# Row sums with 128 columns of ones, a two-row product ahead of GpSimd's solve, and two 64-row halves that take turns

## The chip, the cores and the metric

The kernel runs on one core of a Trainium2 chip (trn2). The metric is the device time of one execution in microseconds (us); smaller is better. The engines are named as the profile names them: PE (TensorE matmul), PEld (its weight loads), DVE (VectorE), ACT (ScalarE), POOL (GpSimd), SP (SyncE, which issues most DMAs).

## What is computed

A decoder trunk of two layers for 256 tokens of width 1024, in float32. The reference, cut to what matters here:

```python
for l in range(DEPTH):                                   # DEPTH = 2
    h = h + 0.5 * swiglu_ffn(rms_norm(h, g[l, 0]), w_in[l, 0], w_out[l, 0])   # width 2816
    u = rms_norm(h, g[l, 1]); z = u @ mix_w_in[l]
    y_a = rwkv7_time_mix(z[..., :1792], ...)             # 8 heads of 64, a recurrence over tokens
    y_b = retention_mix(z[..., 1792:4864], ...)          # 8 heads, chunks of 128 tokens
    h = h + (gate_a * (y_a @ w_branch_a[l]) + gate_b * (y_b @ w_branch_b[l])) @ mix_w_out[l]
    h = h + memory_cross_attn(rms_norm(h, g[l, 2]), mem, ...)
    h = h + 0.5 * swiglu_ffn(rms_norm(h, g[l, 3]), w_in[l, 1], w_out[l, 1])
return rms_norm(h, final_norm)
```

The recurrence of `rwkv7_time_mix` is done in two chunks of 128 tokens. Within a chunk it needs products of keys with queries (scores, masked to the causal half), and the inverse of a unit triangular matrix for each head.

## The kernel before, in words

**Dense products.** Each weight block is fetched by an SP DMA (`raw`), cut by ACT into a rounded part `wh` and by DVE into the rest `wl` (lines 245 and 246), and PE then makes three products of hi and lo parts, a triple (`mm3`): hi by hi, hi by lo, lo by hi. Most are 128 x 128 weights against 256 columns (`unit_k`, `acc_t`; tiles g, u, acc, z, xq), some against 512 columns (`unit`; z). Some 90% of PE's instructions are such triples, one behind the other.

**The order.** PE's order is the one in which the program emits it. `Em` keeps a clock of its own, `em.now`, which each matmul advances by an assumed cost (`mm`), and small tasks cut into the dense stream when their times on that clock have come. So an assumed cost decides between which triples a small product stands. The other engines' orders come from a scheduler that starts from this program.

**Row sums.** `norm` runs ahead of each of the eight sublayers: two float32 matmuls of `ss` (squares, 128 x 128) by one column of `s.ones` add the squares of a token's row. The result `rb` goes through DVE, POOL (a power) and ACT, and comes back as a second pair of matmuls (`rb<-diagh`, `rb<-diagl`). `rw_low` has four such one-column products per layer (`dsc`). A float32 matmul is two instructions on PE.

**The solve.** `rw_chain` runs once per layer. PE makes scores `sc` of `be` and `al`, ACT copies them to `U`, SP DMAs carry them through DRAM (`ug`) into `us`, and POOL inverts 64 triangular blocks by 31 steps of a product and a sum (lines 1179 and 1180). Step k works on k // 2 + 1 rows of 31 - k elements, so from step 2 on it has two rows or more. `xs` starts as a constant (line 1171) that is loaded long before. The result goes through DRAM again (`xg`, `XB`), and PE needs `XB` for the first `SA` product, which stands in PE's queue behind a number of dense z products.

**The scores of keys.** `late(t)`, called for t = 0 ahead of that first `SA` and for t = 1 behind the first chunk, makes the products `sc<-mh,kh` and so on. Heads stand in pairs, one on partitions 0 to 63 and one on 64 to 127, so each product uses 64 rows of PE's array. The loop is over the half `o` outside, then over `i` and `pr`, with `mm3` inside: all 12 products of a half come together and the other half follows after some z products. DVE masks each bank into `S` (line 1143).

Of the kernel before, what the change touches and what calls it, by code (L numbers as in the profile page):

```python
# [13 lines left out]
AF = mybir.ActivationFunctionType  # L14
# [10 lines left out]
def make_consts():  # L25
    f = np.float32
    i = np.arange(P)
    c = {}
    c["ident"] = np.eye(P, dtype=f)
    # cum[s, t] = (s <= t) - (s <= 63): inclusive running sum centred on the middle of the chunk  # L30
    c["cum"] = (i[:, None] <= i[None, :]).astype(f) - (i[:, None] <= 63).astype(f)
    ms = np.zeros((P, 2, P), np.int32)
    ms[:, 0, :] = np.where(i[:, None] < i[None, :], -1, 0)
    ms[:, 1, :] = np.where(i[:, None] <= i[None, :], -1, 0)
    c["masks"] = ms
    half = CDEC * 0.5
    b = np.zeros((P, 8), np.float64)
    b[:, 0] = -half * (i - 63)
    b[:, 1] = half * (i - 63)
    b[:, 2] = -half * (i - 64)  # L40
    b[:, 3] = -CDEC * 64
    b[:, 4] = i >= 64
    b[:, 5] = i < 64
    b[:, 6] = -0.5
    c["cols"] = b.astype(f)
    lg = np.log1p(-np.exp2(-5.0 - np.arange(8, dtype=np.float64)))
    t = np.arange(256, dtype=np.float64)[:, None]
    gam = np.stack([np.exp(t * lg), 0.125 * np.exp(-t * lg)], 1)  # [256, 2, 8]
    c["gam"] = np.ascontiguousarray(gam.reshape(2, P, 2, 8).transpose(1, 0, 2, 3)).astype(f)
    # angles: inverse frequencies and 1/(2 pi) cut into four 12-bit pieces  # L50
    fr = (10000.0 ** (-np.arange(32) / 32)).astype(f)
    pieces = []
    from fractions import Fraction
    inv2pi = Fraction(15915494309189533576888376337251436203445964574046, 10 ** 50)
    r = inv2pi
    e = -3
    for _ in range(4):
        q = Fraction(int(r * Fraction(2) ** (11 - e)), 1) / Fraction(2) ** (11 - e)
        pieces.append(float(q))
        r -= q  # L60
        e -= 12
    c["freq"] = np.broadcast_to(np.concatenate([fr, fr]).astype(f), (P, 64)).copy()
    c["_pieces"] = pieces
    x0 = np.zeros((P, 16, 32), f)
    for p in range(P):
        for rr in range(16):
            x0[p, rr, 2 * rr + p // 64] = 1.0
    c["x0"] = x0
    return c
# [7 lines left out]
class Em:  # L77
    """Emits the program: the dense products are the main stream, the other tasks cut in when ready."""
# [83 lines left out]
class K:  # L162
# [63 lines left out]
    def hp(s, gen):  # L226
        """a task whose steps go before others on the other engines"""
        while True:
            with s.tc.high_priority():
                try:  # L230
                    y = next(gen)
                except StopIteration:
                    return
            yield y
# [57 lines left out]
    def unit(s, X, key, K, c, ps):  # L292
        """ps[t][128 tok, c] = x W for a block of columns of W, K row blocks."""
        k = 0
        while k < K:
            wh, wl = s.W.next(key)
            for j in range(wh.shape[1]):
                if X == s.Xu:
                    yield s.ev_u[k // 2]
                for t in range(2):  # L300
                    s.mm3(ps[t][:, :c], *X(t, k), wh[:, j, :], wl[:, j, :], k == 0, k == K - 1)
                yield 0
                k += 1
            s.W.done()

    def unit_k(s, X, key, K, nc_, ps):
        """ps[c // 2][:, c % 2] = (x W)^T for nc_ blocks of 128 columns: the weights stand, the tokens move.
        Two groups share a bank: its first product alone clears the bank."""
        k = 0
        while k < K:  # L310
            wh, wl = s.W.next(key)
            for j in range(wh.shape[1]):
                if X == s.Xt:
                    yield s.ev_u[k // 2]
                xh, xl = X(k)
                for c in range(nc_):
                    o = ps[c // 2][:, c % 2 * 256:c % 2 * 256 + 256]
                    cs = slice(c * P, (c + 1) * P)
                    s.mm3(o, wh[:, j, cs], wl[:, j, cs], xh, xl, k == 0 and c % 2 == 0, k == K - 1 and c % 2 == 1)
                    if c % 2:  # L320
                        yield 0
                k += 1
            s.W.done()

    def acc_t(s, X, key, k0, nk, acc, start):
        """acc[j][:, i] += (x[k0:k0+nk] W rows)^T for column blocks 2j + i, a chunk being one row block by 1024 columns."""
# [11 lines left out]
    def acc_t_last(s, parts, acc, done):  # L338
        """The last row blocks of an accumulation, bank by bank; done(j) follows each."""
# [14 lines left out]
    def acc_chunk(s, X, key, k0, nk, acc, start):  # L354
        """acc[t][n] += x[k0:k0+nk] W rows, by tokens"""
# [11 lines left out]
    def acc_last(s, parts, acc, scale):  # L367
        """the last row blocks, token tile by token tile, and the final norm"""
# [24 lines left out]
    def prep(s, j):  # L393
        """blocks 2j, 2j + 1 of h are final"""
# [29 lines left out]
    def norm(s, ss, ev, early, wait):  # L424
        """half of 1/rms, for the token of a partition and along the free axis of every partition"""
# [4 lines left out]
        for t in range(2):  # L430
            s.mm(b[:, t:t + 1], ss[:, 0, t * P:(t + 1) * P], s.ones[:, 0:1], True, True)
# [7 lines left out]
        with s.tc.high_priority():  # L439
            nc.vector.tensor_scalar(x, b[:, 0:2], 4.0 / D, 4e-6, ALU.mult, ALU.add)  # L440
# [35 lines left out]
    def start(s):  # L476
        """x transposed into the trunk, the first weights and the first u"""
# [36 lines left out]
    def hl(s, src, name):  # L514
        """[128, 512] -> hi and lo parts"""
# [11 lines left out]
    def transp(s, src, t, pr):  # L527
        """[128, 512] of tokens by columns -> the four transposed blocks in hi and lo parts (a PE step)"""
# [96 lines left out]
    def h_tok(s):  # L625
        """the trunk of the last sublayer, by tokens"""
# [53 lines left out]
    def fin(s, acc, scale):  # L680
        """done(j) for acc_t_last: blocks 2j, 2j + 1 of h get their sum"""
# [43 lines left out]
    def evac(s, ps, name, free=True):  # L725
        """z = u W with 1/rms applied, for both token tiles"""
# [138 lines left out]
    # RWKV-7: decay, gate and in-context rate from the low-rank columns  # L865
    def rw_low(s, l, ps):
# [85 lines left out]
        for b in range(4):  # L952
            s.mm(pd[:, b:b + 1], tm[:, b * P:(b + 1) * P], s.ones[:, 0:1], True, True)
        s.ar.free(tm)
        R["dsc"] = s.sm.tile([P, 4], F32, name="dsc", tag="dsce")
        act.activation(R["dsc"], pd[:, 0:4], AF.Exp, scale=-hc, bias=s.col(3))
# [17 lines left out]
    def shift(s, z):  # L974
        """the rows of the token before"""
# [10 lines left out]
    def shift_mix(s, z, zs, mu):  # L986
        """z + (z of the token before - z) mu, in place"""
# [143 lines left out]
    def scores(s, lT, rT):  # L1131
        """[s, t] products, the even heads in one bank and the odd heads in another"""
# [13 lines left out]
    def rw_chain(s, l):  # L1146
# [19 lines left out]
        # unit upper triangular 32 x 32 diagonal blocks inverted, one (token tile, head, block) and  # L1166
        # every other row to a partition
# [3 lines left out]
        nc.gpsimd.dma_start(xs, A["x0"])  # L1171
        for i in range(2):
# [18 lines left out]
        def late(t):  # L1191
# [18 lines left out]
            for o in range(2):  # L1210
# [3 lines left out]
                KQ[t][o] = []  # L1214
                p0, p1 = 64 * o, 64 * o + 64
                for i in range(2):
                    b = s.ps.alloc("sc")
                    for pr in range(2):
                        f = lambda x: x[p0:p1, pr].rearrange("p c t -> p (c t)")
                        s.mm3(b[:, pr * 256:pr * 256 + 256], kh[p0:p1, 2 * i + pr, :], kl[p0:p1, 2 * i + pr, :],  # L1220
                              f(mv[i][0]), f(mv[i][1]), True, True)
                    x = s.ar.alloc("S", F32, (P, 2, 2, P))
                    s.mask_evac(x, b, s.masks.unsqueeze(1).broadcast_to([P, 2, 2, P]))
# [89 lines left out]
    # retention  # L1313
# [121 lines left out]
    def mem_t(s):  # L1435
        """the memory times 1/rms of its rows, transposed, into DRAM"""
# [30 lines left out]
    def mem_prep(s, l):  # L1467
        """the normalised memory, transposed, in hi and lo parts: blocks of [128, 2, 256]"""
# [17 lines left out]
    def mem_v(s, n):  # L1486
        """half of the memory's values"""
# [47 lines left out]
    def x_scores(s, n, qT, kT, sc, pT, ev):  # L1535
        """softmax over the memory for heads 2n, 2n + 1, and its transpose"""
# [36 lines left out]
    def x_out(s, n, pT, vv, oT, evp, ev):  # L1573
        """the transposed output of heads 2n, 2n + 1 in hi and lo parts"""
# [98 lines left out]
```

## Time and profile before

| | |
|---|---|
| median of 3 runs | 1536.84 us (1536.01 to 1538.4) |
| profiled execution, first to last instruction (span) | 1535.5 us |
| PE busy | 98% of the span |
| DVE, ACT, POOL busy | 69%, 50%, 10% |
| granted TensorE clock, mean | 0.989 |

The profile shows one execution. Its own time beyond the span is not given; the runs that make the median were timed apart and lie 1.3 us above the span. A PE matmul row gives the start and a modelled duration that overlaps the next one; the pace of a stretch is read from the starts, or from the chain of waits, which gives the time of a stretch and the number of its matmuls.

### The profile page before, as it was taken

Reading aid. Unit: us, or ns where it says so; the run is one execution under the profiler, and the core shown is the slowest. Engines: PE = TensorE matmul, PEld = TensorE weight load, DVE = VectorE, ACT = ScalarE, POOL = GpSimd, SP = SyncE. Lnnn points to the kernel's source line nnn. Section 1 sums busy time; section 2 is a strip of 40 time slices with the busy share of each in tenths; the row PEclk is TensorE's granted clock in tenths of the full one; section 3 lists DMA queues with packets and bytes.
Section 4 is the critical chain, followed back from the end, with each engine's and each line's share of the span. In section 5 each row is a group of like instructions: output and inputs, shape, how many; then the busy total and the mean of one; then the engine's idle time right before and its main releaser. Section 6 shows DMA issues by size and latency. Waiting matters only on the chain.

```text
span 1535.5 us, 28618 instructions
## 1 busy us (share of the span) xinstructions
PE 1501.5 (98%) x11763; PEld 1427.0 (93%) x11763; DVE 1055.8 (69%) x1459; ACT 766.7 (50%) x1053; POOL 152.4 (10%) x229
## 2 busy tenths in 40 slices
PE   8999999989999999999999999999799999999998
PEld 8999988868999999999999999888699999999997
DVE  7966599947646767665685666899466477576664
ACT  6554465525434555444464444654354356464442
POOL 4010001370000000000001000205600000000000
PEclk9999999998999999999999999999899999999999
DMA  8677656525445545666567554564354454466661
GB/s 278 218 225 241 195 170 195 172 65 189 152 147 162 189 127 188 192 193 193 178 209 228 188 189 156 192 213 144 117 165 139 152 177 167 137 197 193 194 195 46
DMA packets 143066, 271.19 MB, mean 177 GB/s; under 512 B 22580, under 2 KB 35108, under 8 KB 142936
## 3 DMA queue, kind: packets, MB, share of 16 engines
q1 hardware_dynamic: 139560, 261.12, 52.9%
q0 software_dynamic: 2864, 7.63, 1.9%
q8 instruction: 92, 1.51, 0.4%
q10 hardware_dynamic: 512, 0.62, 0.1%
q14 instruction: 38, 0.31, 0.1%
HBM read 263.05 MB, written 3.15 MB: 173 GB/s over the span
## 4 chain that ended last, share of the span: by engine, by line
PE 89%; POOL 5%; DMA 2%; issue 1%; SPq 1%; DVE 1%; ACT 1%; POOLq 0%
PE z L211 25%; PE acc L211 21%; PE g L211 16%; PE u L211 16%; POOL tm L1179 3%; PE xq L211 3%; POOL xs L1180 2%; PE tp L223 1%; PE SA L211 1%; PE Y L211 1%; PE G L211 1%; PE xo L211 1%; PE xs L211 1%; SPq L1164 1%; PE sc L211 1%
## 5 line engine op out<-in xcount | busy, mean ns | idle before, releaser
L246 DVE TENSOR_TENSOR wl<-raw,wh 128x1024 fp32r<-128x1024 f32 x476 | 582.0, 1230 | 310.2 <-ACT wh L245 308.2
L245 ACT ACTIVATE wh<-raw 128x1024 fp32r<-128x1024 f32 x476 | 501.3, 1059 | 538.6 <-PE z L211 145.6
L211 PE MATMUL g<-uh,wh 128*128 128x256 f32 x704 | 196.8, 280 | 0.0
L211 PE MATMUL g<-uh,wl 128*128 128x256 f32 x704 | 196.5, 279 | 0.0
L211 PE MATMUL g<-ul,wh 128*128 128x256 f32 x704 | 196.5, 279 | 0.0
L211 PE MATMUL u<-uh,wh 128*128 128x256 f32 x704 | 196.3, 279 | 0.0
L211 PE MATMUL u<-uh,wl 128*128 128x256 f32 x704 | 195.8, 278 | 0.0
L211 PE MATMUL u<-ul,wh 128*128 128x256 f32 x704 | 195.7, 278 | 0.0
L211 PE MATMUL acc<-ah,wh 128*128 128x256 f32 x528 | 146.9, 278 | 0.0
L211 PE MATMUL acc<-ah,wl 128*128 128x256 f32 x528 | 146.8, 278 | 0.0
L211 PE MATMUL acc<-al,wh 128*128 128x256 f32 x528 | 146.8, 278 | 0.0
L211 PEld LDWEIGHTS g<-uh,wh 128*128 128x128 f32 x704 | 134.0, 190 | 0.2
L211 PEld LDWEIGHTS g<-uh,wl 128*128 128x128 f32 x704 | 133.1, 189 | 0.1
L211 PEld LDWEIGHTS g<-ul,wh 128*128 128x128 f32 x704 | 133.0, 189 | 0.2
L211 PEld LDWEIGHTS u<-uh,wh 128*128 128x128 f32 x704 | 132.9, 189 | 0.0
L211 PEld LDWEIGHTS u<-uh,wl 128*128 128x128 f32 x704 | 132.4, 188 | 0.0
L211 PEld LDWEIGHTS u<-ul,wh 128*128 128x128 f32 x704 | 132.3, 188 | 0.0
L211 PE MATMUL z<-wh,uh 128*128 128x512 f32 (+1 forms) x320 | 125.4, 392 | 0.0
L211 PE MATMUL z<-wh,ul 128*128 128x512 f32 (+1 forms) x320 | 122.4, 383 | 0.4 <-DVE ul L407 0.4
L211 PE MATMUL z<-wl,uh 128*128 128x512 f32 (+1 forms) x320 | 121.6, 380 | 0.0
L211 PEld LDWEIGHTS acc<-ah,wh 128*128 128x128 f32 x528 | 99.9, 189 | 0.0
L211 PEld LDWEIGHTS acc<-ah,wl 128*128 128x128 f32 x528 | 99.2, 188 | 0.0
(400 smaller groups left out, 3331.5 us busy)
## 6 DMA issues: line engine op xcount, KB each, us to landing
raw<-in_ffn_w_in SPq DMA_DIRECT2D x176, 512.0 KB, 4.4
raw<-in_mix_w_in SPq DMA_DIRECT2D x108, 512.0 KB, 4.4
raw<-in_ffn_w_out SPq DMA_DIRECT2D x88, 512.0 KB, 4.3
raw<-in_cross_w_kv SPq DMA_DIRECT2D x32, 512.0 KB, 3.6
raw<-in_w_branch_b SPq DMA_DIRECT2D x16, 512.0 KB, 3.6
raw<-in_mix_w_out SPq DMA_DIRECT2D x16, 512.0 KB, 3.6
raw<-in_cross_w_q SPq DMA_DIRECT2D x16, 512.0 KB, 3.9
raw<-in_cross_w_o SPq DMA_DIRECT2D x16, 512.0 KB, 4.2
```

The source lines that it names most:

```text
L211: s.nc.tensor.matmul(out, l, r, start=start, stop=stop)
L223: s.nc.tensor.transpose(out, src, s.ident)
L245: s.nc.scalar.activation(hi, src, AF.Copy)
L246: s.nc.vector.tensor_tensor(lo, src, hi.bitcast(F32), ALU.subtract)
L1164: nc.sync.dma_start(ugv[t, k][:, q], U[t][q][32 * k:32 * k + 32, :, 32 * k:32 * k + 32])
L1179: nc.gpsimd.tensor_tensor(tm[:, 0:nr, 0:w], xc, row, ALU.mult)
L1180: nc.gpsimd.tensor_tensor(xs[:, 0:nr, k + 1:32], xs[:, 0:nr, k + 1:32], tm[:, 0:nr, 0:w], ALU.add)
```

## The change

Three edits. In `norm` and `rw_low` the right operand `s.ones[:, 0:1]` becomes all 128 columns of `s.ones`, and the readers take every 128th column. Behind the load of `xs`, POOL runs one product of two rows by 29 elements on `xs`, written to `tm` where the solve overwrites it. In `late`, the loop over `i` is outside now and the loop over the half `o` innermost, so the products of the two halves alternate, in two banks; `em.now` is set back by 650 ns after each 12.

```diff
 in norm
-            s.mm(b[:, t:t + 1], ss[:, 0, t * P:(t + 1) * P], s.ones[:, 0:1], True, True)
+            s.mm(b[:, t * P:(t + 1) * P], ss[:, 0, t * P:(t + 1) * P], s.ones, True, True)
...
-            nc.vector.tensor_scalar(x, b[:, 0:2], 4.0 / D, 4e-6, ALU.mult, ALU.add)
+            nc.vector.tensor_scalar(x, b[:, 0:2 * P:P], 4.0 / D, 4e-6, ALU.mult, ALU.add)
 in rw_low
-            s.mm(pd[:, b:b + 1], tm[:, b * P:(b + 1) * P], s.ones[:, 0:1], True, True)
+            s.mm(pd[:, b * P:(b + 1) * P], tm[:, b * P:(b + 1) * P], s.ones, True, True)
...
-        act.activation(R["dsc"], pd[:, 0:4], AF.Exp, scale=-hc, bias=s.col(3))
+        act.activation(R["dsc"], pd[:, 0:4 * P:P], AF.Exp, scale=-hc, bias=s.col(3))
 in rw_chain
         nc.gpsimd.dma_start(xs, A["x0"])
+        nc.gpsimd.tensor_tensor(tm[:, 0:2, 0:29], xs[:, 0:2, 2:3].broadcast_to([P, 2, 29]),
+                                xs[:, 2:3, 3:32].broadcast_to([P, 2, 29]), ALU.mult)
 in rw_chain, late
-            for o in range(2):
+            KQ[t][:] = [], []
+            for i in range(2):
                 yield 1776.0
                 yield from s.psneed(2)
                 yield from s.arneed(2)
-                KQ[t][o] = []
-                p0, p1 = 64 * o, 64 * o + 64
-                for i in range(2):
-                    b = s.ps.alloc("sc")
-                    for pr in range(2):
-                        f = lambda x: x[p0:p1, pr].rearrange("p c t -> p (c t)")
-                        s.mm3(b[:, pr * 256:pr * 256 + 256], kh[p0:p1, 2 * i + pr, :], kl[p0:p1, 2 * i + pr, :],
-                              f(mv[i][0]), f(mv[i][1]), True, True)
+                b = [s.ps.alloc("sc") for _ in range(2)]
+                for pr in range(2):
+                    for n, (x, y) in enumerate(((kh, 0), (kh, 1), (kl, 0))):
+                        for o in range(2):
+                            p0, p1 = 64 * o, 64 * o + 64
+                            s.mm(b[o][:, pr * 256:pr * 256 + 256], x[p0:p1, 2 * i + pr, :],
+                                 mv[i][y][p0:p1, pr].rearrange("p c t -> p (c t)"), n == 0, n == 2)
+                s.em.now -= 650.0
+                for o in range(2):
                     x = s.ar.alloc("S", F32, (P, 2, 2, P))
-                    s.mask_evac(x, b, s.masks.unsqueeze(1).broadcast_to([P, 2, 2, P]))
+                    s.mask_evac(x, b[o], s.masks.unsqueeze(1).broadcast_to([P, 2, 2, P]))
                     KQ[t][o].append(x)
```

The order of the instructions moves at three places. On PE, the first 12 products of the keys' scores in the first layer (`sc` with its number is the bank) stood, in their first seven:

```order
L211 MATMUL sc_3623<-mh_3555,kh_3551 128x256
L211 MATMUL sc_3623<-ml_3556,kh_3551 128x256
L211 MATMUL sc_3623<-mh_3555,kl_3552 128x256
L211 MATMUL sc_3623<-mh_3555,kh_3551 128x256
L211 MATMUL sc_3623<-ml_3556,kh_3551 128x256
L211 MATMUL sc_3623<-mh_3555,kl_3552 128x256
L211 MATMUL sc_3632<-mh_3557,kh_3551 128x256
```

and stand now, in their first six:

```order
L211 MATMUL sc_3624<-mh_3556,kh_3552 128x256
L211 MATMUL sc_3625<-mh_3556,kh_3552 128x256
L211 MATMUL sc_3624<-ml_3557,kh_3552 128x256
L211 MATMUL sc_3625<-ml_3557,kh_3552 128x256
L211 MATMUL sc_3624<-mh_3556,kl_3553 128x256
L211 MATMUL sc_3625<-mh_3556,kl_3553 128x256
```

Each bank belongs to one half now, and every instruction uses the other half than the one ahead of it. There are 12 in a group, as before, and two groups per call of `late`.

On PE, some 45 z products ahead of the first `SA` (the lines left out are of the same kinds):

```order
-L211 MATMUL z<-wh,uh 128x512
-L211 MATMUL z<-wl,uh 128x512
-L211 MATMUL z<-wh,ul 128x512
...
+L211 MATMUL z<-uh,wh 128x256
+L211 MATMUL z<-ul,wh 128x256
+L211 MATMUL z<-uh,wl 128x256
```

Six products of 512 columns stand earlier than here and 12 of 256 columns come in from behind the solve's consumers: in each layer PE has 12 z products of 256 columns more ahead of the first `SA`, and as many fewer later.

On POOL, around the solve of the first layer, before:

```order
L1171 DMA xs<-in_x 128x512
L250 DMA rk<-in_a_r_k 128x512
L250 DMA ln_3583<-in_a_ln 128x512
L250 DMA ln_3585<-in_a_ln 128x512
L250 DMA gn<-in_b_gn 128x512
L1179 TENSOR_TENSOR tm<-xs,us 128x31
L1180 TENSOR_TENSOR xs<-xs,tm 128x31
```

and now:

```order
L1171 DMA xs<-in_x 128x512
L1172 TENSOR_TENSOR tm<-xs 128x2x29
L250 DMA rk<-in_a_r_k 128x512
L250 DMA ln_3584<-in_a_ln 128x512
L250 DMA ln_3586<-in_a_ln 128x512
L1181 TENSOR_TENSOR tm<-xs,us 128x31
L250 DMA gn<-in_b_gn 128x512
L1182 TENSOR_TENSOR xs<-xs,tm 128x31
```

The added product stands far ahead, behind the load of `xs`, and the issue of the `gn` load now stands inside the solve, behind its first product. DVE's order at that time, after the change:

```order
L1124 TENSOR_TENSOR C_3588<-C_3588,ln_3586 128x512
L1119 TENSOR_TENSOR zv<-zv,vm 128x512
L1125 TENSOR_TENSOR C_3588<-C_3588,g 128x512
L1124 TENSOR_TENSOR C_3594<-C_3594,ln_3586 128x512
L1143 TENSOR_TENSOR S<-sc,masks 128x512 x2
L1126 TENSOR_TENSOR g<-g,ln_3584 128x512
L1125 TENSOR_TENSOR C_3594<-C_3594,g 128x512
L246 TENSOR_TENSOR wl<-raw,wh 128x1024
L1126 TENSOR_TENSOR g<-g,ln_3584 128x512
L246 TENSOR_TENSOR wl<-raw,wh 128x1024 x3
L1004 TENSOR_REDUCE bvm<-bv 128x4 x2
```

The two masks `S` stand three instructions later in this run than before; what follows them is still a closed run of sums and products on tiles in SBUF, of seven instructions.

## Rows read from the trace of the kernel before

**Rows 1.** The page's first part: busy us, share and instructions by engine.
```profile
PE 1501.5 (98%) x11763; PEld 1427.0 (93%) x11763; DVE 1055.8 (69%) x1459; ACT 766.7 (50%) x1053; POOL 152.4 (10%) x229
```
**Rows 2.** Waits of PE: engine line waited for, us in total, times, longest.
```profile
PE SA L211 <- DMA XB<-xg: 19.7, 2, 9.8
```
**Rows 3.** Chain of waits around the first solve: start us, us, what.
```profile
344.50 3.63 DMA XB<-xg
```
**Rows 4.** Clock by windows: us, busy PE PEld DVE ACT POOL, PEclk, DMA.
```profile
338.00:359.00 21.00, 11.16 (x68) 10.43 (x68) 16.52 (x25) 8.04 (x11) 5.54 (x6) 0.60 0.85 248
```
**Rows 5.** Timeline of PE, scores: start us, us, engine line op out<-in.
```profile
400.87 1.16 PE L211 MATMUL sc<-qT,beT 64*128 64x128 f32 x16
401.96 0.38 PE L211 MATMUL z<-uh,wh 128*128 128x256 f32 x1
404.21 0.38 PE L211 MATMUL sc<-mh,kh 64*128 64x256 f32 x1
...
404.44 0.28 PE L211 MATMUL sc<-ml,kh 64*128 64x256 f32 x1
...
405.84 0.39 PE L211 MATMUL z<-uh,wh 128*128 128x256 f32 x1
```
**Rows 6.** Timeline of POOL: loads ahead of the solve, its slow steps, both layers.
```profile
247.43 0.61 POOL L1171 DMA_DIRECT2D xs<-in_x  x1 [8.76 <-PE cum L211]
273.04 0.54 POOL L250 DMA_DIRECT2D rk<-in_a_r_k  x1 [25.00 <-PE tp L223]
...
297.72 8.40 POOL L1179 TENSOR_TENSOR tm<-xs,us 128x58 f32<-128x58 f32 x1
307.31 1.26 POOL L1179 TENSOR_TENSOR tm<-xs,us 128x81 f32<-128x81 f32 x1
...
1056.46 8.40 POOL L1179 TENSOR_TENSOR tm<-xs,us 128x58 f32<-128x58 f32 x1
```
**Rows 7.** Timeline of DVE over the same stretch of the first layer.
```profile
297.73 0.69 DVE L1119 TENSOR_TENSOR zv<-zv,vm 128x512 f32<-128x512 f32 x1
...
302.48 3.50 DVE L246 TENSOR_TENSOR wl<-raw,wh 128x1024 fp32r<-128x1024 f32 x3
305.88 1.28 DVE L1004 TENSOR_REDUCE bvm<-bv 128x4 f32<-128x512 f32 x2
...
307.17 1.21 DVE L246 TENSOR_TENSOR wl<-raw,wh 128x1024 fp32r<-128x1024 f32 x1
```
**Rows 8.** Timeline of PE: small float32 products in the dense stream.
```profile
782.91 0.50 PE L211 MATMUL rb<-ones,sq 128*128 128x1 f32 x4
783.27 0.36 PE L211 MATMUL u<-uh,wh 128*128 128x256 f32 x1
...
326.27 1.17 PE L211 MATMUL O<-bv,rS 128*128 128x128 f32 x9
327.20 0.48 PE L211 MATMUL z<-wh,uh 128*128 128x512 f32 x1
```
**Rows 9.** Chain of waits, dense stretches: start us, us, what, number of matmuls.
```profile
25.39 7.88 PE u L211 x66
...
94.51 0.44 PE tp L223 x4
94.95 10.22 PE acc L211 x90
...
540.34 0.87 PE tp L223 x8
541.21 4.24 PE xq L211 x36
...
611.71 10.88 PE g L211 x96
...
783.41 5.76 PE u L211 x48
...
939.22 16.96 PE acc L211 x144
```

## The prediction: what the time becomes

> **What bounds the kernel now.** I read the busy shares first. PE is busy 98% of the span [rows 1]; no other engine comes near, so PE's own pace and the places where PE stands still decide. Then PE's waits: one line holds almost everything, two waits of 9.8 us, one per layer, for `XB`, the result of POOL's solve [rows 2]. Followed back along the chain, `XB` lands at 348.1 in the first layer [rows 3], behind POOL's 62 steps. The windows show a second cost: over the 21 us around that wait the granted clock averages 0.60 [rows 4], that is a stretch at the lower of TensorE's two levels (1.2 against 2.4 GHz), which came while PE stood idle and lasts into the work behind it. Last, the pace of the dense stream. It has two values: 96 products of 256 columns take 10.88 us at 611.71, or 113.3 ns each, but 144 take 16.96 us at 939.22, or 117.8 ns [rows 9]. Each value holds for long stretches at the full clock and changes only where something small cuts in.
>
> **Sum 1: the halves that take turns.** A group of 12 key products lasts 1.63 us (404.21 to 405.84), at about 0.12 us each after the first step [rows 5]. The scores `sc<-qT,beT` already alternate the halves: 16 instructions in 1.09 us (400.87 to 401.96), 68 ns each [rows 5], where nine float32 instructions that use all rows take 0.93 us, 103 ns each (326.27 to 327.20, [rows 8]). So two halves run side by side. Six pairs in place of 12 products save six steps of 0.12: 0.71 us a group, 8 groups. The price of switching cannot eat this, since the alternating scores pay it too; the bounds are 0 (products of 256 columns don't overlap) and 0.8 (half of a group). Four groups belong to t = 1 and lie in a PE that waits for nothing: 4 x 0.71 = 2.8 us gained. The four of t = 0 lie ahead of the wait for `XB`: what they save, 1.43 us a layer, PE would only wait longer. But 12 products of 256 columns now stand ahead of the first `SA` in their place, 12 x 0.1133 = 1.36 us a layer, taken from the work behind the wait: 2.7 us gained.
>
> **Sum 2: the solve.** The added product is meant to run where POOL has nothing: between the load of `xs` at 247.43 and the next load at 273.04 [rows 6]. Even if it needed 10 us there, nobody waits for it, and it costs nothing. Does it take anything away? The first two-row step takes 8.40 us in both layers, while a larger one 9 us later takes 1.26 [rows 6]. DVE explains it: from 297.73 to 305.98 it works without a gap on instructions that read two tiles from SBUF, the last three of them `wl<-raw,wh` [rows 7]. POOL's step begins at 297.72 and ends at 306.12, 0.14 us behind that run, when DVE has gone on to a sum over one input. The step at 307.31 ends at 308.57, 0.19 us behind `wl`, which ends at 308.38 [rows 6, 7]. So I take the 8.40 for a lockout by DVE, which a product 40 us earlier does not touch, and its gain for 0. The closed run on DVE is still there after the change, in seven instructions rather than ten; with two masks ahead of it, which read PSUM, other steps of the solve get through and another is caught. New on the chain is the issue of `gn` between two steps, 0.54 us by the like load [rows 6]. I charge 0.6 us a layer, between 0 (hidden in the lockout) and 1.5 (with one more `wl` of 1.21 us, [rows 7], that catches a step): 1.2 us lost.
>
> The Trainium skill ("GPSIMD Engine Reference", section 2.1) says that the first call to a freshly loaded GpSimd kernel pays about 6 us for code, with no instruction of its own in the profile. By that the sum would gain, not lose; it is rival A.
>
> **Sum 3: 128 columns.** Four instructions of one column take 0.36 us (782.91 to 783.27), 90 ns each; the nine `O` instructions of 128 columns take 103 each [rows 8]. By that pair 48 instructions cost 48 x 0.013 = 0.6 us more; the bounds are 0 and, if each paid another whole step, 48 x 0.103 = 5 us. The `O` row has the form of the new sums and is nearest, but its first and last steps touch other products; I take 0.3, which is lost in the rounding of the sum. The Trainium skill ("TensorE: Matmul & The Clock Gate", Back-to-back issue gap) lists 60 cycles for up to 64 columns and 134 for 128; by it, as an estimate, 48 instructions would cost 1.5 us more, where the pair of rows gives 0.6.
>
> What the width may change is the pace behind it. Behind the one-column sums the stream runs slow in the rows I have at 25.39 (66 in 7.88 us, 119) and 783.41 (48 in 5.76, 120), although the stretch that leads up to the second began fast at 611.71 [rows 9]; the slow pace then lasts from 783 to 956, 173 us. Behind four transposes, which move 128 columns like the new sums, 90 products take 10.22 us, 113.6; behind eight, 36 take 4.24, 117.8 [rows 9]. Four instructions of 128 columns are what `rb` now is, so I put the fast pace behind it as the likelier. Then 173 x (1 - 113.3 / 117.8) = 6.6 us go in that stretch. From 25 to 89 it is 0.8 to 2.4 us, depending on whether other small products at 46 keep the pace; 0.5 us for the shorter pieces. I take 8.5 us. The stretch at 611.71 is fast already.
>
> **The total.** 2.8 + 2.7 - 1.2 - 0.3 + 8.5 = 12.5 us from a span of 1535.5. The median of the runs, 1536.84, lies 1.3 us above the span; the same difference carries over: 1524. DVE, ACT and SP get other orders in places, as for the masks; all work that they do then is behind queues with buffers, PE waits for none of it today [rows 2], and I charge nothing. If that cover is gone, `SA`, `G` and their copies would show as PE waits, some tenths of a us each, 14 such steps a layer: up to 3 us.
>
> **Rivals.** **A, the lockout is code after all:** the added product takes the first-use cost. For: both layers show the same 8.40 to the hundredth, always at the first two-row step. Against: DVE's closed run ends with it [rows 7]. `XB` would come 2 x 8.1 us sooner and PE's idle time shrink to some 2 us, too short to lose all of the clock: with half-rate work of 2 to 4 us a layer saved, some 21 us more than my sum: 1503. **B, the width leaves the pace as it was:** one sum in a triple stream upsets it, wide or not. Then only 4.3 us stay: 1532.5. **C, the fast pace comes but does not hold:** 3.5 us behind each `rb` a second pair of products follows, and one of the two long stretches (611 to 780 and 783 to 956) is slow behind it. That costs about 6.6 us of the sum: 1531. **D, slower:** the width leaves the row sums slow, and the second pair no longer turns the stretch from 611 to 780 back to the fast pace, which it did before; 169 us x 4% = 6.7 us lost against 4.3 gained: 1539. It decides at 611.71: 10.88 us for 96 products, or 11.31. That the halves do not overlap after all would take 4 us from any case.
>
> **How the numbers follow.** About 0.2%, 3.1 us, is what a measurement of this kernel can tell from no change. My forecast 0.42; C 0.18; B 0.20; D 0.10; A 0.06; the rest, 0.04, for waits that I don't see. My forecast, C and A are faster, B mostly so (4.3 us, but 2 with the upper charge for the solve), D slower: faster 0.78, same 0.09, slower 0.13. The range takes in C, B and D, and below my forecast the clock around `XB`, which may come back earlier, and a halves' gain at its bound: 1515 to 1540. My forecast's own range is 1519 to 1529.
>
> **What would show it.** Right: key groups of 0.9 us in the chain; PE's two waits for `XB` still 9 to 11 us; a POOL step of 5 us or more still there, ending with a DVE run; `rb` still 0.36 us a group, with 113 ns behind it at 783 and 611. Wrong: waits for `XB` of 2 us (A), 117.8 ns at 783 (B, C) or at 611 (C, D), key groups of 1.6 us, or new lines in PE's waits.

## The result: 1548.58 us, slower by 0.8%, and the profile after

The changed kernel takes 1548.58 us (median of 4 runs, 1546.12 to 1551.76) against 1536.42 of the kernel before (1534.05 to 1538.4). The ratio is 1.0078, 95% interval 1.0063 to 1.0094. The forecast was 1524.0, with a range of 1515 to 1540. The profiled execution has a span of 1550.0 us, 14.5 more than before. The four runs fall in two pairs, near 1546 and near 1551; the profiled one is of the upper pair, so the accounts below explain 14.5 us and not the 12.2 between the medians.

PE has as many instructions as before and is busy 3.1 us less [rows 1], so the time lies in waits. The kernel after, first part of the page:

```profile
PE 1498.4 (97%) x11763; PEld 1423.1 (92%) x11763; DVE 1057.9 (68%) x1459; ACT 763.4 (49%) x1053; POOL 162.6 (10%) x231
```

Waits of PE after (line waited for: us in total, times, longest):

```profile
PE SA L211 <- DVE yb L1409: 21.0, 2, 10.6
PE G L211 <- ACT SA L1267: 11.1, 2, 5.7
...
PE z L211 <- ACT yaTh L245: 2.0, 2, 1.0
PE z L211 <- DVE yaTl L246: 1.9, 2, 0.9
```

Before there was only the wait for `XB` [rows 2]. Now the same first `SA` waits for a DVE instruction, `yb`, and the longer wait is not the whole loss: `G`, the next product of the chain, waits 5.5 us in each layer, and two z products one behind the other wait 1.95 us together in each.

Where the time went, by stretches. Each number is the difference of the time between the same two PE instructions in the two traces, worked out from their starts:

| stretch | first layer, us | second layer, us |
|---|---|---|
| start and first FFN; for the second layer the FFNs around 783 to 963 | -0.5 | -6.3 |
| up to the first `SA` | +0.7 | +0.6 |
| first `SA` to the second, with `G` between | +6.5 | +8.1 |
| key scores of t = 1 | -1.4 | -1.4 |
| behind the last `Y`, up to the next FFN | +4.0 | +4.0 |

Together these are the 14.3 us by which the last row sum comes later. Two forecasts came in: the key scores save 1.4 us a layer, and the long stretch from 783 on runs fast. In the 173 us from 783 to 956 PE ran 1529 matmuls, where it had run 1471. Windows of the kernel before, then after:

```profile
783.00:956.00 173.00, 173.00 (x1471) 173.00 (x1470) 107.81 (x121) 80.47 (x95) 7.40 (x17) 1.00 0.61 197
```

```profile
783.00:956.00 173.00, 173.00 (x1529) 173.00 (x1528) 112.45 (x127) 82.10 (x97) 7.41 (x17) 1.00 0.66 209
```

The loss starts on ACT. Its timeline after, around the first solve (start us, us, what, idle before and what ended it):

```profile
343.45 1.06 ACT L245 ACTIVATE wh<-raw 128x1024 fp32r<-128x1024 f32 x1 [24.82 <-DMA raw<-in_mix_w_in]
344.41 2.04 ACT L1404 ACTIVATE yb<-O 128x512 f32<-128x512 f32 x4
...
354.51 0.63 ACT L245 ACTIVATE kh<-kaT 128x512 fp32r<-128x512 f32 x1 [7.12 <-DVE yb L1421]
...
359.02 0.57 ACT L1267 ACTIVATE SA<-SA 32x512 f32<-32x512 f32 x1
```

ACT stands 24.82 us for one weight load. Behind it in ACT's queue are the four squares `yb<-O`, whose inputs had been there for 17 us (PE's last `O` product is followed by the next z at 326.69). Why the load is late stands in SP's queue after:

```profile
335.89 1.31 SPq L1185 DMA_DIRECT2D xg<-xs  x2
337.29 1.43 SPq L256 DMA_DIRECT2D raw<-in_mix_w_in  x2
342.29 0.37 SPq L1187 DMA_DIRECT2D XB<-xg  x1
```

SP cannot issue the store `xg` before POOL's last step (it ends at 335.86), and the load of `raw` comes behind that store. `XB` landed at 345.91, earlier than the 348.13 of before [rows 3], but `SA` could not start yet. The chain of the rest is in DVE's timeline after:

```profile
344.54 1.23 DVE L246 TENSOR_TENSOR wl<-raw,wh 128x1024 fp32r<-128x1024 f32 x1 [23.45 <-ACT wh L245]
345.68 0.68 DVE L1004 TENSOR_REDUCE bss<-yb 128x4 f32<-128x512 f32 x1
...
347.71 0.69 DVE L1409 TENSOR_TENSOR yb<-O,brn 128x512 f32<-128x512 f32 x1 [1.15 <-POOL brn L263]
```

The first `yb<-O,brn` ends at 348.40 and frees a PSUM bank; `SA` starts at 348.51. The other three follow until 356, each over DVE, POOL and DVE again; ACT's `kh` waits for a product on one of them, which ends at 354.48, and the copy of `SA` that `G` needs stands behind `kh` and three `wh`. It ends at 359.59, and `G` starts:

```profile
359.65 1.91 PE L211 MATMUL G<-SA,U 32*32 32x64 f32 x16 [5.44 <-ACT SA L1267]
```

PE's second stop costs clock too. At half the clock PE was from 342 to 359 before; after, it fell, came back for 3.4 us while PE stood before `G`, and fell again. Windows of before, then of after (PEclk is the third number from the end):

```profile
342.00:359.00 17.00, 10.73 (x64) 10.20 (x65) 14.73 (x23) 8.04 (x11) 3.83 (x3) 0.50 0.90 284
```

```profile
339.90:353.60 13.70, 5.09 (x31) 4.96 (x32) 6.38 (x12) 3.94 (x6) 3.42 (x3) 0.50 0.82 258
353.60:357.00 3.40, 0.61 (x5) 0.40 (x3) 2.50 (x5) 2.49 (x4) 1.31 (x1) 0.99 0.00 0
357.00:367.30 10.30, 7.65 (x43) 7.48 (x44) 10.17 (x14) 4.26 (x7) 0.00 (x0) 0.50 0.65 191
...
493.40:497.00 3.60, 3.60 (x20) 3.60 (x19) 0.00 (x0) 0.72 (x1) 0.00 (x0) 0.53 0.35 124
```

The last of these windows belongs to the second loss, behind the last transposes of a layer. Timeline of PE there, before:

```profile
484.05 0.60 PE L223 MATMUL tp<-ident,y 128*128 128x128 f32 x4
484.40 0.48 PE L211 MATMUL z<-wh,memh 128*128 128x512 f32 x1
...
485.86 0.28 PE L211 MATMUL z<-yaTh,wh 128*128 128x256 f32 x1
```

and after:

```profile
489.39 0.60 PE L223 MATMUL tp<-ident,y 128*128 128x128 f32 x4
490.97 0.39 PE L211 MATMUL z<-yaTh,wh 128*128 128x256 f32 x1 [0.98 <-ACT yaTh L245]
```

Six z products stood between the transposes and the product that needs them. The 12 z products that were moved ahead of `SA` are missing at this end, the stream closed up, and nothing covers ACT's and DVE's copies any more. PE waits 1.95 us; 3.6 us at a clock of 0.53 follow, 1.7 us of lost work; and the 319 products of 256 columns behind them, up to the next row sum, ran at 117.8 ns and not at 113.3 as before, 1.4 us. Less the 1.4 us that the 12 products took, that makes some 3.7 of the 4.0 us.

### The profile page after: what moved, and what is told of

Its sections match the earlier page's. It is cut to its first block, busy times and chain, and to the rows that moved or that the text cites. A ratio compares the mean times of both kernels' runs of the same rounds, so it can differ in the third digit from the quotient of the medians.

```text
span 1550.0 us, 28634 instructions
## 1 busy us (share of the span) xinstructions
PE 1498.4 (97%) x11763; PEld 1423.1 (92%) x11763; DVE 1057.9 (68%) x1459; ACT 763.4 (49%) x1053; POOL 162.6 (10%) x231
## 4 chain that ended last, share of the span: by engine, by line
PE 86%; POOL 5%; DVE 4%; ACT 2%; issue 1%; DMA 1%; SPq 0%; POOLq 0%; ACTq 0%; DVEq 0%
PE z L211 25%; PE acc L211 20%; PE u L211 16%; PE g L211 15%; PE xq L211 3%; POOL xs L1182 2%; POOL tm L1181 2%; PE tp L223 1%; PE Y L211 1%; DVE wl L246 1%; PE SA L211 1%; PE G L211 1%; ACT wh L245 1%; DMA raw<-in_mix_w_in 1%; PE xo L211 1%
## 5 line engine op out<-in xcount | busy, mean ns | idle before, releaser
L211 PEld LDWEIGHTS acc<-al,wh 128*128 128x128 f32 x528 | 99.2, 188 | 0.0
```

The costliest lines, as they stand in the source:

```text
L211: s.nc.tensor.matmul(out, l, r, start=start, stop=stop)
```

## Experiments

The first theory: the 650 ns by which the change sets the planner's clock back are to blame, since they move the 12 products, and with them a second `wh` ahead of the squares. Rivals: the wide sums, or the added product. The first four runs do each edit alone, and the whole without the set-back.

**Row sums alone.**

```diff
-            s.mm(b[:, t:t + 1], ss[:, 0, t * P:(t + 1) * P], s.ones[:, 0:1], True, True)
+            s.mm(b[:, t * P:(t + 1) * P], ss[:, 0, t * P:(t + 1) * P], s.ones, True, True)
...
-            s.mm(pd[:, b:b + 1], tm[:, b * P:(b + 1) * P], s.ones[:, 0:1], True, True)
+            s.mm(pd[:, b * P:(b + 1) * P], tm[:, b * P:(b + 1) * P], s.ones, True, True)
```

> Only the row sums change, 128 columns in place of one. Theory 'keeps': a sum of 128 columns leaves the dense stream at the pace that it finds, where a sum of one column always leaves it slow. So 783 to 956 us runs at 113.3 ns a product (117.8 before): 6.3 us gained there, 0.8 in the first FFN, nothing at 602 and 1359, where the stream is slow already: 7 us below the kernel before, 1529 to 1530, and PE's waits for XB stay at 9.8 us twice. Rival 'width is to blame' (the wide sums bring the loss of the whole change): over 1540, with new lines in PE's waits.

Measured: 1530.91 us, 0.9955 of before (0.994 to 0.997). The stretch from 783 on gains 6.4 us, by the same reckoning as above, the first FFN 0.8, the waits around `SA` give some back. The wide sums are a gain.

**The added product alone.**

```diff
+        nc.gpsimd.tensor_tensor(tm[:, 0:2, 0:29], xs[:, 0:2, 2:3].broadcast_to([P, 2, 29]),
+                                xs[:, 2:3, 3:32].broadcast_to([P, 2, 29]), ALU.mult)
```

> Only the two-row product ahead of the solve is added. Theory 'first use': it takes 8.4 to 8.8 us itself, the solve's step with 128x58 elements falls from 8.40 to about 0.6, and the steps behind it, which then run beside DVE's closed run, lose 3 to 4 us of that again; the solve ends some 4 us sooner, PE's waits for XB fall to 5 to 7 us, and the time to 1526 to 1529. Rival 'lockout by DVE' (that of the prediction): the added product takes under 1 us, 8.40 stays in the solve, time 1536 to 1537. Rival 'the added product brings the loss of the whole change' (POOL late for others): over 1540.

Measured: 1536.18 us, 0.9994 (0.9982 to 1.0005): nothing. The trace of the whole change had made me turn to 'first use' before this run, since the added product took 8.82 us there and the step of 128x58 fell to 0.62. That reading falls here. POOL's timeline of this run, second layer:

```profile
1010.08 7.05 POOL L1172 TENSOR_TENSOR tm<-xs 128x58 f32<-128x58 f32 x1 [4.89 <-DVE kk L1046]
...
1054.54 0.24 POOL L1182 TENSOR_TENSOR xs<-xs,tm 128x30 f32<-128x30 f32 x1
1054.86 8.40 POOL L1181 TENSOR_TENSOR tm<-xs,us 128x58 f32<-128x58 f32 x1
```

The added product takes 7.05 us, and 45 us later the solve's step takes its 8.40 all the same. The row sums alone show the reverse, a solve in the second layer with no long step and no product ahead of it. POOL, row sums alone:

```profile
1052.86 1.10 POOL L1180 TENSOR_TENSOR xs<-xs,tm 128x30 f32<-128x30 f32 x1
1054.04 0.62 POOL L1179 TENSOR_TENSOR tm<-xs,us 128x58 f32<-128x58 f32 x1
1054.73 1.15 POOL L1180 TENSOR_TENSOR xs<-xs,tm 128x58 f32<-128x58 f32 x1
1055.96 0.61 POOL L1179 TENSOR_TENSOR tm<-xs,us 128x56 f32<-128x56 f32 x1
```

And the added product of the whole change, 251.32 to 260.14, ends 0.15 us behind a closed run of DVE. That run, from 251.69 on, and what follows it:

```profile
251.69 0.69 DVE L1080 TENSOR_TENSOR qt<-zr,E 128x512 f32<-128x512 f32 x1
...
256.50 3.49 DVE L246 TENSOR_TENSOR wl<-raw,wh 128x1024 fp32r<-128x1024 f32 x3
259.91 0.69 DVE L1331 TENSOR_TENSOR ra<-z,rot 128x512 f32<-128x512 f32 x1
```

In all twelve profiles (before, after and ten runs), 20 steps of the solve and the ten added products take over 5 us, and each of these 30 ends 0.1 to 0.2 us behind such a run of DVE, with `wl` as its last instruction. The steps have 31, 30 or 58 elements and stand anywhere from the first to the fifth, so two rows have nothing to do with it. All this is as a lockout by DVE would have it and not as a first use would; no run moved DVE's closed run by itself.

**The halves alone, with the set-back.**

```diff
+                for pr in range(2):
+                    for n, (x, y) in enumerate(((kh, 0), (kh, 1), (kl, 0))):
+                        for o in range(2):
...
+                s.em.now -= 650.0
```

> Only the halves of the key scores alternate, with the 650 ns set back. Theory 'set-back': 12 z products stand ahead of the first SA, ACT has a second wh ahead of the four squares yb, and that wh waits for a load which SP issues only behind the solve's result. Then SA waits for a PSUM bank that yb holds, some 12 to 14 us in each layer, G waits 5 us more for ACT, the z behind the last transposes waits 2 us: with the old solve and the old pace 1553 to 1562, slower than the whole change. Rival 'the loss comes from another part': two groups of t = 1 save 0.71 us each in each layer, 1531 to 1535, waits of SA still for XB.

Measured: 1541.27 us, 1.0027 (1.0017 to 1.0037). Slower, but far less than expected. The waits behind the transposes are there (2.0 us for ACT's copy and 1.9 for DVE's, both layers together); the next run, without the set-back, has none, so they do come from the set-back. No wait at `G`. ACT's timeline of this run:

```profile
321.76 1.06 ACT L245 ACTIVATE wh<-raw 128x1024 fp32r<-128x1024 f32 x1 [3.00 <-PE z L211]
322.72 0.58 ACT L1402 ACTIVATE yb<-O 128x512 f32<-128x512 f32 x1
```

The squares run 22 us earlier than in the whole change, though the same number of `wh` stands ahead of them. So my first theory was short of something.

**The whole change without the set-back.**

```diff
-                s.em.now -= 650.0
```

> The whole change without the line that sets the clock back by 650 ns; the halves still alternate. Theory 'set-back': ACT has one wh ahead of yb as before, SA waits for XB and not for yb, no wait of 5 us at G and none of 2 us behind the transposes; the pace gains 7 us, the key scores of t = 1 save 2.9 us, the solve gives 2 to 4 us a layer: 1517 to 1523, faster than both kernels. Rivals 'the row sums or the added product bring the loss': 1540 or more, with the waits of the whole change.

Measured: 1525.71 us, 0.9924 (0.9909 to 0.994): no wait at `G`, none behind the transposes. It is 3 us above what I expected: the solve gives nothing in the first layer (the steps take 39.6 us in place of 41.9 but begin 2.5 us later, and `SA` starts at 348.22, before at 348.27). In both layers `SA` starts 0.14 us behind the landing of `XB`, as before. Against the whole change this run is 22.9 us faster, about what the stretches of the table above lost around `SA` and behind the last `Y`, 22.6 us.

**What was missing** shows when weight loads are counted in the orders of the kernels. In the first layer, up to the store `xg` on SP, and up to the squares `yb` on ACT:

| kernel | loads on SP ahead of `xg` | `wh` on ACT ahead of `yb` |
|---|---|---|
| before; row sums alone; added product alone; whole without set-back | 108 | 108 |
| halves alone, or with the added product | 109 | 109 |
| whole change, with or without the added product | 108 | 109 |

Only in the whole change does ACT need, ahead of `yb`, a load that SP holds behind the solve's result. It takes the set-back (one more `wh`) and the wide sums (one load less ahead of `xg` than the halves alone have) together. The second layer has the same differences, at 346 and 347. That is the second theory, 'load behind the solve', and the next three runs test it.

**The whole change with the sums left at one column.** The edit is the first diff above, undone.

> The whole change with the row sums left at one column. Theory 'load behind the solve': what makes the whole change slow is that the 109th weight load stands behind the store xg of the solve's result on SP while the wh that reads it stands ahead of the squares yb on ACT; here SP's order has that load ahead of xg. So no wait of 5 us at G, SA starts 10 us after the solve's last step, the two waits of 2 us behind the transposes stay: 1538 to 1543, as for the halves alone. Rival 'the set-back with the added product': G waits 5 us or more, 1546 to 1551.

Measured: 1541.83 us, 1.0041 (1.0027 to 1.0055), no wait at `G`. As expected.

**The whole change without the added product.** The edit is the second diff, undone.

> The whole change without the added product. Theory 'load behind the solve': orders of PE, ACT, DVE and SP are those of the whole change, so G waits 5 to 6 us in each layer and SA starts 12 us or more after the solve's last step: 1545 to 1552. Rival 'the added product brings the loss, or it saves 8 us in the solve': 1536 or less in the first case, over 1556 in the second.

Measured: 1551.86 us, 1.0108 (1.0095 to 1.0121). The median is 3.3 us above that of the whole change, the profiled run 0.7 us above its profiled run; what makes the difference of the medians is open. Its waits are those of the whole change:

```profile
PE SA L211 <- DVE yb L1407: 23.1, 2, 12.3
PE G L211 <- ACT SA L1265: 10.9, 2, 5.8
```

**The whole change, with POOL issuing the store.** If the load only waits behind the store, taking the store off SP must free it, with the orders of PE, ACT and DVE as they are.

```diff
-            nc.sync.dma_start(xgv[q], xs[q * 64:(q + 1) * 64])
+            nc.gpsimd.dma_start(xgv[q], xs[q * 64:(q + 1) * 64])
```

> The whole change, but POOL issues the store xg of the solve's result and SP does not: every other order on PE, ACT and DVE stays. Theory 'load behind the solve': load 109 no longer waits for the solve, the squares yb run on ACT some 15 us earlier, the waits of 5 us at G go, SA follows XB; 5 to 7 us gained in each layer, 1533 to 1540. Rival 'the order on ACT and DVE alone costs the time': 1545 or more.

Measured: 1534.37 us, 0.9985 (0.9973 to 0.9997), 14 us below the whole change. The squares start at 322.00, and PE's waits are:

```profile
PE SA L211 <- DMA XB<-xg: 17.9, 2, 9.1
...
PE G L211 <- ACT SA L1267: 2.9, 2, 1.5
```

So the second theory holds: one place in SP's queue lets `SA` wait for `yb` in place of `XB`, and makes some 4 of the 5.5 us at `G`; the other 1.4 stay. Not all of the 14 us are the freed load, for the store on POOL also shortens the way from the solve's last step to `SA`: 8.2 and 8.1 us in the two layers, before 10.2 and 9.7. That is up to 4 us, so 10 us at the least are the freed load. The wide sums tell of it another way: they save 0.45% on the kernel before, and where they also put the load behind the store they cost 0.37% with the added product and 0.81% without it. By that swing, as an estimate, the place in the queue costs 13 to 19 us.

**Row sums and halves, without set-back and added product.**

> Row sums of 128 columns and alternating halves, without set-back and without the added product. Theory 'lockout by DVE': the added product buys nothing, the solve takes 38 to 42 us with or without it; within 3 us of the kernel with it, 1523 to 1529. Rival 'first use': one step of 8 us more in each solve, 1533 or more.

Measured: 1525.36 us, 0.9933 (0.992 to 0.9946), with the added product 1525.71. The product is worth nothing here. In the first layer of this run, with no such product ahead, the step of 128x58 takes 6.56 us. In the first layer of the whole change without the product the lockout falls on another step, and that of 128x58 takes 0.29. POOL there:

```profile
298.39 6.47 POOL L1179 TENSOR_TENSOR tm<-xs,us 128x30 f32<-128x30 f32 x1
304.94 0.24 POOL L1180 TENSOR_TENSOR xs<-xs,tm 128x30 f32<-128x30 f32 x1
305.26 0.29 POOL L1179 TENSOR_TENSOR tm<-xs,us 128x58 f32<-128x58 f32 x1
```

**The same, with the store on POOL.** The two best edits together: the diff of the run with the store, without set-back and added product.

> Row sums of 128 columns and alternating halves, no set-back, no added product, and POOL issues the store xg. From the kernel without set-back and added product (1525.4) the way from the solve's last step to SA falls from 10.3 to 8.1 us as in the run with the store on POOL: 2 us a layer, less about 1 if the solve's steps meet a longer run of DVE: 1520 to 1524. Rival: loads that come sooner put more of DVE's work beside the solve and take it back: 1525 or more.

Measured: 1529.32 us, 0.9958 (0.9943 to 0.9972): a miss, worse than 1525.36. From the solve's last step to `SA` it does take 8.1 us in both layers. It is given back: the solve begins 0.6 to 0.9 us later behind the row sums of its layer, `G` waits 1.5 us in each layer for ACT's copy of `SA`, which stands behind `kh` and three `wh` (`kh` waits for a `yb` until 348.19), and 1.6 us of the difference lie in the first FFN, whose pace from 46 on was slow in this run and fast in the other, with the same instructions. The run without set-back (with or without the product) stays the best, 0.7% faster than the kernel before and 1.5% than the change.

**Sums of 32 columns.** The row sums alone, those of `norm` with 32 columns, and their reader takes every 32nd.

```diff
-            s.mm(b[:, t * P:(t + 1) * P], ss[:, 0, t * P:(t + 1) * P], s.ones, True, True)
+            s.mm(b[:, t * 32:t * 32 + 32], ss[:, 0, t * P:(t + 1) * P], s.ones[:, 0:32], True, True)
```

> As the kernel with the row sums alone, but the sums of the norms have 32 columns (those of dsc keep 128). Theory 'keeps needs the full width': 32 columns act as one does, the stream behind the sum at 783 is slow (117.8 ns): 1534 to 1537. Rival 'anything wider than one column keeps the pace': 113.3 ns there, 1529 to 1532.

Measured: 1537.38 us, 1.0009 (0.9996 to 1.0022), 0.4 us above the expected range. Behind the sum at 779 the stream is slow, by the chain of waits of this run (start us, us, what, matmuls), first line; with 128 columns, in the whole change, it is fast, second fence:

```profile
788.37 11.31 PE g L211 x96
```

```profile
801.23 10.88 PE g L211 x96
```

Counted over the profiles of before, after and all ten runs, for the five row sums of each with products of 256 columns on both sides (fast is 113.3 ns, slow 117.8):

| columns of the sum | fast stays fast | fast to slow | slow stays slow | slow to fast |
|---|---|---|---|---|
| 1 | 0 | 16 | 4 | 0 |
| 32 | 0 | 4 | 0 | 1 |
| 128 | 23 | 0 | 12 | 0 |

At four of the five sums 32 columns act as one does. The fifth turned a slow stream fast, which one column never did, so the theory holds only in part.

## Why the prediction was wrong, point by point

**The step that failed** is the last paragraph of the sum: "DVE, ACT and SP get other orders in places ... all work that they do then is behind queues with buffers, PE waits for none of it today [rows 2], and I charge nothing", with up to 3 us as its bound. It looked at PE, POOL and DVE and did not follow ACT's and SP's queues, where one `wh` moved past four squares and the store stood ahead of its load. The cost was the change's largest term: the stretch from `SA` to the second `SA` grew by 6.5 and 8.1 us. That an engine holds a buffer is no cover if the load itself is queued behind a wait for a third engine. The rule that 'waits of today' show what can go wrong was the fault: none of these waits existed before. The way to the loss is shown by the runs; why the planner's clock and the wide sums together shift the two queues by one load was not followed.

**Sum 1.** The mechanism and the size of the halves were right: a group takes 0.91 us (0.92 forecast), 1.4 us a layer at t = 1. Chain of waits, before and then after:

```profile
404.28 1.63 PE sc L211 x12
```

```profile
411.04 0.91 PE sc L211 x12
```

The other half of the sum, 12 z products "taken from the work behind the wait: 2.7 us gained", was wrong in sign. They were taken from the cover of the last transposes; that end is 4.0 us a layer longer. I priced what the products save and not what they had been hiding.

**Sum 2.** Lockout rather than first use was right, and so was that the added product would cost nothing where it stands (8.82 us, nobody waits) and give nothing. The profile had the reason in it [rows 6, 7]. That "another is caught" was too simple: in the whole change no step was, POOL's steps went through between DVE's instructions at 0.6 to 1.3 us each, and the solve took 38.5 us in place of 41.9, with 0.58 us for the issue of `gn` (0.6 charged). POOL after:

```profile
299.94 0.62 POOL L1181 TENSOR_TENSOR tm<-xs,us 128x58 f32<-128x58 f32 x1
300.64 1.15 POOL L1182 TENSOR_TENSOR xs<-xs,tm 128x58 f32<-128x58 f32 x1
```

That gain reached nobody, as `SA` then waited for `yb`. The Trainium skill ("GPSIMD Engine Reference", section 8) says that GpSimd shares its SBUF interfaces with VectorE and contends with DVE instructions of two SBUF inputs. The traces agree, with steps of 0.24 to 0.6 us that last 5.6 to 8.4. The Trainium skill's rule on the first call (section 2.1 there), cited ahead, is not what acted here: 0.29 us for the first two-row step, above.

**Sum 3.** The width costs nothing between dense products: four instructions take 0.36 us with 128 columns as with one [rows 8]. PE after:

```profile
792.23 0.61 PE L211 MATMUL rb<-ones,sq 128*128 128x128 f32 x4
792.59 0.37 PE L211 MATMUL u<-uh,wh 128*128 128x256 f32 x1
```

That the stretch from 783 would be fast was right, 6.3 us against 6.6. The reason given, that four instructions of 128 columns set the fast pace, was not: they leave the pace as it is, fast or slow. So the 1.5 us that I hoped for from 25 on became 0.8, and the stretch at 611 did not change.

**The rivals.** None of A to D came: the 8.40 was no code, the stretch from 783 is fast, and so is that from 611. C's distance was misread as well: the second pair stands 4.6 to 8.2 us behind the sum, not 3.5. The slower outcome had 0.13, by way of D; the one that came, a load held back behind the solve on SP, was none of mine, and only the 0.04 "for waits that I don't see" has room for it.

## What to carry to other kernels

When a planner's clock or a size moves work, follow every in-order queue through the point where one engine waits long for another, and count: does any engine there need, ahead of work that others want, a load that is queued behind that wait? Here 108 against 109 decided over 10 us, and the clock setting that made it, together with the wide sums, looked like a tuning constant. Work pulled forward to fill one wait is taken from the cover of another place, so price both ends.

## What was not expected of the hardware

The pace of the dense stream has two values that last for 150 us and more at the full clock, and small float32 products move it between them: a sum of one column always left it slow (20 of 20), one of 128 columns never changed it (35 of 35), one of 32 did either. With the same instructions on PE the first FFN, from 46 on, was fast in one run and slow in another, so the order alone does not fix the pace. What holds it is open; no run tried it.

POOL beside DVE shows two modes: a step of 0.24 us lasts to the end of DVE's run (5.6 to 8.4 us), or the steps slip in between DVE's instructions at 0.6 to 1.3 us each, as in the second layer of the row sums alone. What decides which comes stays open.

Two stops of PE of 1 us each, before 490.97 and 492.29, had 3.6 us at a clock of 0.53 behind them, from 493.4 on, where PE had been at full clock through the stops themselves.
